# Attention and recurrent stage of a decoder layer: a scheduler's order, and one written out by hand

## The chip, the core and the metric

The kernel runs on one core of one Trainium2 chip. A core has a matrix engine (TensorE, PE in the profile; its weight loads are listed as PEld), VectorE (DVE), ScalarE (ACT), GpSimd (POOL) and SyncE (SP), which here only issues transfers (DMAs). Each engine works through its own list of instructions in order and waits on semaphores for the others. The metric is the device time of one execution in microseconds (us), the median of several runs.

## The reference, cut to what matters

One layer is computed for a prompt of 512 tokens and for 8 single decode tokens, so every activation has 520 columns here. Ahead of the second half of the layer (a mixer of experts, which the change does not touch) stand two branches that read the same normalized input `h`:

```
mods = jax.nn.silu(c) @ w_ada + b_ada
h = rms_norm(x, norm1_w) * (1 + sc1) + sh1
qa, ka, va, qh, fh, ih, gh, ga, gb = jnp.split(h @ w_in, IN_OFFSETS, axis=-1)
...
qa = rms_norm(qa.reshape(att_shape), q_norm_w) * (ATT_HEAD_DIM ** -0.5)
ka = rms_norm(ka.reshape(att_shape), k_norm_w)
att, kv_rows = attend(qa, ka, va)
f = lb + (1 - lb) * jax.nn.sigmoid(fh.astype(jnp.float32))
q_hg = jax.nn.silu(qh.astype(jnp.float32)).reshape(hg_k_shape)
k_hg = (1 - f).reshape(hg_k_shape)
logf = jnp.log(f).reshape(hg_k_shape)
o_hg, hg_state = recur(q_hg, k_hg, v_hg, logf)
o_hg = rms_norm(o_hg, hg_norm_w) * jax.nn.silu(gh.astype(jnp.float32).reshape(B, T, HG_HEADS, HG_DV))
y = jax.nn.sigmoid(ga) * (att @ w_br_a) + jax.nn.sigmoid(gb) * (hg @ w_br_b)
x = x + g1 * (y @ w_o)
```

`attend` is windowed attention in three groups of 8 heads of 64; `recur` is a gated linear recurrence with 8 heads of 128x128 state.

## The kernel before, in words

The product `h @ w_in` is done in column blocks of 128: 36 blocks for attention (four pairs of heads `hp`, three groups `g`, q, k and v), 32 for the recurrence (eight heads, each f, q, v and the output gate gg) and 16 for the two merge gates. One block, called a product here, is `proj`: a 512 KB weight tile `raw` is loaded, split into a rounded part `whi` (ACT, L129) and the rest `wlo` (DVE or POOL, L130), and 48 matmuls (8 chunks of the 1024 rows, three combinations, two halves of 260 columns) add up in a pair of PSUM banks (L177).

Stages, in order of time. First the modulation vectors and `h`. Then attention: for each head pair nine products, the norms of q and k (`norm_bc`: square on ACT, a rounded split, four matmuls, a square root on ACT, a reciprocal over 128x520 on DVE, L308, a multiplication), and eight slots (`r`, `hh`; L382 to L413). A slot computes scores with four matmuls S (L386 to L389), masks and takes their maximum on DVE (L392, L394), the exponential on ACT (L397), scales by the reciprocal sum (DVE, L400), transposes six pieces T (L404, L407) and multiplies with the values V (L411, L413). Sixteen blocks of the modulation weights (`mods`, "slabs", two half tiles each, L209 to L213) are given out beside the slots. Then the recurrence: each head's four products are followed by a chain: a logarithm, a running sum (`bb`), seven levels of decays (two subtractions L570, L571, an exponential L572, two multiplications L573, L574, matmuls L584, a masked copy L592), the state (L598 to L608), the decode states of 8 tokens on POOL (L617 to L619), the head's output `ob` and its norm. Decode attention (L417 to L475) stands once, before head 4. Last come the merge (`w_br_a`, `w_br_b`), `w_o` and the expert mixer.

Up to the mixer a scheduler sets each engine's order: it takes the program's order as priority and places instructions where it expects an engine to be free. From `order_.__enter__()` (L715) on, in the mixer, the engines' order is that of the program text (`manual_schedule`).

Of the kernel before, what the change touches and what calls it, by code (L numbers as in the profile page):

```python
# [36 lines left out]
MH = (0,) * 8  # L37
# [8 lines left out]
GT = ((0,),(1,),(2,),(3,),(),(4,),(5,),(6,))  # L46
GL = (7,)
# [3 lines left out]
NB_ = dict(sq=1, rs=2, shi=2, slo=2)  # L51
# [31 lines left out]
def layer(ctx, tc, A, O, K):  # L83
# [203 lines left out]
    def hblk(name):  # L287
        return hb.tile([P, N], F32, tag="hb", name=name, bufs=12)

    def wcol(c0):  # L290
        return A["w_in"][c0 // P]

    def norm_bc(x, lhsT, w, pl):

        sq, rs = pl("sq", F32), pl("rs", F32)
        act.activation(sq, x, AF.Square)
        parts = [sq]
        if lhsT.dtype == F32R:
            parts = pl("shi", F32R), pl("slo", F32R)
            split(*parts, sq, pool)  # L300

        def finish():
            for s in range(2):
                ps = bank("pn")
                for i, t in enumerate(parts):
                    pe.matmul(ps[:, :NH], lhsT, t[:, s * NH:(s + 1) * NH], start=i == 0, stop=i == len(parts) - 1)
                act.activation(rs[:, s * NH:(s + 1) * NH], ps[:, :NH], AF.Sqrt, bias=eps)
            dve.reciprocal(rs, rs)  # L308
            dve.scalar_tensor_tensor(out=x, in0=x, scalar=w, in1=rs, op0=ALU.mult, op1=ALU.mult)

        return finish
# [17 lines left out]

    with tc.tile_pool(name="at", bufs=2) as at:  # L330
# [9 lines left out]
        slabs = mods(range(8, 24))  # L340
        for hp in range(4):
            q, k, v, vtm = {}, {}, {}, {}
            for g in range(3):
                for t, dst, w in ((0, q, wq8), (1, k, col(C_K)), (2, v, None)):
                    ps = proj(wcol(t * 1536 + g * 512 + hp * P), KC, hT_hi, hT_lo)
                    x = at.tile([P, N], F32, tag="qkv", name="x", bufs=QKV)
                    act.activation(two(x), half(ps), AF.Copy)
                    if t:
                        finish()
                    if w is not None:  # L350
                        finish = norm_bc(x, bd, w, lambda n, dt: at.tile([P, N], dt, tag=n, name=n, bufs=NB_[n]))
                    dst[g] = x
# [27 lines left out]
            for r in range(4):  # L380
# [34 lines left out]
                for _ in range(MO[hp * 4 + r]):  # L415
                    next(slabs, None)
# [217 lines left out]
    for _ in slabs:  # L634
        pass
# [671 lines left out]
```

## Time and profile before

| | |
|---|---|
| median of 3 runs | 2489.33 us (2483.14 to 2490.37) |
| profiled execution, its own time | 2487.92 us |
| its span, first to last instruction | 2486.1 us |
| busy: PE, DVE, ACT, POOL | 94%, 71%, 46%, 30% of the span |
[...]
| first attention product leaves PSUM | 61.0 us after the span's start |
| first merge product with the recurrence's result | 989.0 us |

Busy PE is not the same as PE at its peak: matmuls overlap in the records, so a stretch can read as full while fewer matmuls go through it. The count of matmuls per stretch and the granted clock say more. [...]

### The profile page before, as it was taken

Reading aid. Unit: us, or ns where it says so; the run is one execution under the profiler, and the core shown is the slowest. Engines: PE = TensorE matmul, PEld = TensorE weight load, DVE = VectorE, ACT = ScalarE, POOL = GpSimd, SP = SyncE. Lnnn points to the kernel's source line nnn. Section 1 sums busy time; section 2 is a strip of 40 time slices with the busy share of each in tenths; the row PEclk is TensorE's granted clock in tenths of the full one; section 3 lists DMA queues with packets and bytes.
Section 4 is the critical chain, followed back from the end, with each engine's and each line's share of the span. In section 5 each row is a group of like instructions: output and inputs, shape, how many; then the busy total and the mean of one; then the engine's idle time right before and its main releaser. Section 6 shows DMA issues by size and latency. Waiting matters only on the chain.

```text
span 2486.1 us, 37938 instructions
## 1 busy us (share of the span) xinstructions
PE 2329.5 (94%) x14547; PEld 2133.4 (86%) x14547; DVE 1763.6 (71%) x3131; ACT 1155.2 (46%) x1801; POOL 738.1 (30%) x490
## 2 busy tenths in 40 slices
PE   8999999998897998999987989989999999999997
PEld 4869798888897998988987889978888888888886
DVE  4646573648786666536898897667888878788876
ACT  3545443555563555233336778733333333333332
POOL 1323120114227212002342000024454445454433
PEclk9989899999996998998998999989999999999999
DMA  7342421235443323432245456679999999999985
GB/s 243 110 141 92 132 89 44 71 96 166 150 126 103 115 91 100 154 105 95 78 129 186 180 187 225 227 272 349 335 349 336 356 329 342 341 348 331 345 298 208
DMA packets 197465, 495.49 MB, mean 199 GB/s; under 512 B 18122, under 2 KB 84650, under 8 KB 195748
## 3 DMA queue, kind: packets, MB, share of 16 engines
q1 hardware_dynamic: 147636, 313.02, 38.0%
q0 software_dynamic: 39456, 143.28, 16.1%
q10 hardware_dynamic: 10192, 36.77, 3.9%
q8 instruction: 114, 1.87, 0.3%
q14 instruction: 67, 0.55, 0.1%
HBM read 439.17 MB, written 54.49 MB: 199 GB/s over the span
## 4 chain that ended last, share of the span: by engine, by line
PE 36%; DVE 7%; issue 6%; ACT 3%; POOL 3%; DMA 1%; ACTq 0%; POOLq 0%; SPq 0%; DVEq 0%
PE acc L1186 16%; PE ph L809 14%; PE pp L177 3%; POOL gat L960 2%; PE pp L1071 2%; ACT oa L1063 1%; DVE wlo L130 1%; ACT whi L129 1%; DVE e L869 1%; ACT stage L1078 1%; DVE y L839 1%; DVE sel L871 0%; PE pt L895 0%; DVE oa L1057 0%; DVE e L866 0%
## 5 line engine op out<-in xcount | busy, mean ns | idle before, releaser
L130 DVE TENSOR_TENSOR wlo<-raw,whi 128x1024 fp32r<-128x1024 f32 (+1 forms) x238 | 293.9, 1236 | 198.5 <-ACT whi L129 196.9
L129 ACT ACTIVATE whi<-raw 128x1024 fp32r<-128x1024 f32 (+1 forms) x284 | 295.2, 1040 | 294.1 <-PE pp L177 168.3
L960 POOL DMA_INDIRECT gat<-in_peer_u,idx x128 | 212.6, 1661 | 627.1 <-DVE junk L987 442.0
L809 PE MATMUL ph<-h_hi,whi 128*128 128x384 f32 x1024 | 355.9, 348 | 15.1 <-ACT whi L129 15.1
L809 PE MATMUL ph<-h_hi,wlo 128*128 128x384 f32 x1024 | 351.6, 343 | 8.0 <-POOL wlo L130 7.3
L809 PE MATMUL ph<-h_lo,whi 128*128 128x384 f32 x1024 | 350.4, 342 | 0.0
L177 PE MATMUL pp<-hT_hi,whi 128*128 128x260 f32 x1344 | 292.5, 295 | 6.0 <-ACT hT_hi L129 4.8
L177 PE MATMUL pp<-hT_hi,wlo 128*128 128x260 f32 x1344 | 288.8, 294 | 1.9 <-DVE wlo L130 1.9
L177 PE MATMUL pp<-hT_lo,whi 128*128 128x260 f32 x1344 | 288.3, 294 | 0.5 <-DVE hT_lo L130 0.5
L177 PEld LDWEIGHTS pp<-hT_hi,whi 128*128 128x128 f32 x1344 | 218.5, 196 | 10.9 <-ACT hT_hi L129 4.9
L177 PEld LDWEIGHTS pp<-hT_hi,wlo 128*128 128x128 f32 x1344 | 218.2, 196 | 4.7 <-DVE wlo L130 2.1
L177 PEld LDWEIGHTS pp<-hT_lo,whi 128*128 128x128 f32 x1344 | 217.7, 197 | 3.5 <-issue 1.8
L809 PEld LDWEIGHTS ph<-h_hi,whi 128*128 128x128 f32 x1024 | 197.4, 193 | 19.5 <-ACT whi L129 16.7
L809 PEld LDWEIGHTS ph<-h_hi,wlo 128*128 128x128 f32 x1024 | 196.6, 192 | 10.2 <-POOL wlo L130 7.9
L809 PEld LDWEIGHTS ph<-h_lo,whi 128*128 128x128 f32 x1024 | 196.6, 192 | 2.8
L1186 PE MATMUL acc<-vhi,chi 128*128 128x512 f32 x768 | 195.8, 390 | 0.0
L1186 PE MATMUL acc<-vhi,clo 128*128 128x512 f32 x768 | 195.0, 389 | 0.0
L1186 PE MATMUL acc<-vlo,chi 128*128 128x512 f32 x768 | 194.9, 389 | 0.0
L130 DVE TENSOR_TENSOR vlo<-vr,vhi 128x1024 fp32r<-128x1024 f32 x128 | 156.2, 1220 | 52.9 <-ACT vhi L129 52.9
L129 ACT ACTIVATE vhi<-vr 128x1024 fp32r<-128x1024 f32 x128 | 135.3, 1057 | 114.7 <-PE acc L1186 114.7
L813 ACT ACTIVATE ge<-ph 128x384 f32<-128x384 f32 x128 | 62.6, 489 | 264.3 <-PE ph L809 263.9
L960 POOL DMA_INDIRECT gat<-in_peer_v,idx x128 | 162.7, 1271 | 70.9 <-issue 34.0
(375 smaller groups left out, 4688.9 us busy)
## 6 DMA issues: line engine op xcount, KB each, us to landing
raw<-in_uT SPq DMA_DIRECT2D x128, 512.0 KB
vr<-in_peer_v SPq DMA_DIRECT2D x128, 512.0 KB
raw<-in_w_in SPq DMA_DIRECT2D x84, 512.0 KB
raw<-in_w_ada SPq DMA_DIRECT2D x48, 512.0 KB
d_G<-stage ACTq DMA_DIRECT2D x12, 2048.0 KB
gt<-d_G SPq DMA_DIRECT2D x32, 768.0 KB
d_ge<-ge ACTq DMA_DIRECT2D x56, 192.0 KB
ge<-d_ge SPq DMA_DIRECT2D x56, 192.0 KB
```

The source lines that it names most:

```text
L129: act.activation(hi, src, AF.Copy)
L130: return (eng or dve).tensor_tensor(out=lo, in0=src, in1=hi.bitcast(F32), op=ALU.subtract)
L177: pe.matmul(ps[:, s, :NH], w[:, k, :], x[:, k, s * NH:(s + 1) * NH], start=first and n == 0, stop=last and n == 2)
L809: pe.matmul(ph[:, :NB], w[:, k], x[:, k, :NB], start=k == 0 and n == 0, stop=k == KC - 1 and n == 2)
L813: act.activation(ge, ph[:, :NB], AF.Gelu_apprx_tanh)
L839: dve.match_replace(out=y[:n], in_to_replace=vals[:, 0:8], in_values=x, imm_value=-3.0e38)
L869: dve.tensor_tensor(out=e3[:n], in0=e3[:n], in1=pb[:n, :, None, :].to_broadcast([n, H, 16, 16]), op=ALU.mult)
L960: pool.indirect_dma_start(out=t, out_offset=None, in_=A[tab][0], in_offset=bass.IndirectOffsetOnAxis(ap=idx, axis=0))
L1063: act.activation(oas[g][:, j], oas[g][:, j], AF.Copy, scale=sels[t][:, 0, n + j:n + j + 1])
L1071: pe.matmul(pgs[g // 2][:, g % 2, j * P:(j + 1) * P], oa[:, j], ob[:, j], start=True, stop=True)
L1078: act.activation(st[:, :, n0:n0 + 8], pgs.pop(b).rearrange("p s (n i) -> p i (s n)", i=P), AF.Copy)
L1186: pe.matmul(acc[2 * t + d], a[:, t * P:(t + 1) * P], b[:, d * 512:(d + 1) * 512], start=first and n == 0, stop=last and n == 2)
```

## The change

From the first attention product to the end of the recurrence the order is now the program's own (`flow = tc.manual_schedule`), and the program is written anew for it. A list `plan` names the weight tiles in the order of use; `weights_in` loads three tiles ahead and splits two ahead, always on ACT and DVE. Between any two products one step of other work is placed (`beside`): a slot of the previous head pair, divided into S in one step, T in the next and V after both heads; one norm's second part; or one of ten pieces of a recurrent head's chain, with the chains of two heads under way at once; beside them one or two steps of decode attention (`step_all`). Transfers of results are put off to the next step (`after`). The four first merge-gate blocks go between attention's last slots, the others into the heads, and none is left behind the recurrence.

Smaller edits go with it: sigmoid times x is computed as half of (tanh of half x plus 1) times x, where the halves go into later factors; `f` and `k` are made on ACT instead of DVE; the finest of the seven levels takes `f` itself (`neighbours`) and needs no decay; the decode states move from POOL (three operations of 128x1024 per head) to ACT and DVE (8 each of 128x128); the square root takes all 520 columns at once. Further on, where the mixer begins, the transposes that carry rows out are issued ahead of the matmuls that they used to interrupt, and their copies between ACT's other work.

```diff
-GT = ((0,),(1,),(2,),(3,),(),(4,),(5,),(6,))
-GL = (7,)
+
+
+G0 = 4
+GT = tuple((G0 + h,) for h in range(7)) + (tuple(range(G0 + 7, 16)),)
...
+    flow = tc.manual_schedule(engines={x.engine for x in (pe, dve, act, pool, dma)})
+    flow.__enter__()
...
+    for hp in range(4):
+        for n, (t, g) in enumerate(FIRST):
+            plan.append((acol(t, g, hp), KC))
+            if hp == 0 or hp == 1 and n < 7:
+                plan += slab_plan(8 + 9 * hp + n)
+    plan += [(hcol(i, 0), KC) for i in (1, 0, 2, 3)] + [(gcol(i), KC) for i in range(G0)]
+    for h in range(8):
+        plan += [(hcol(i, h + 1), KC) for i in (1, 0, 2, 3)] if h < 7 else []
+        plan += [(gcol(i), KC) for i in GT[h]]
...
+    def weights_in():
+
+        k = at_[2]
+        at_[2] += 1
+        while at_[0] < min(len(plan), k + 4):
+            src, kc = plan[at_[0]]
+            parts[at_[0]] = wtile("raw", F32, RAW)
+            dma.dma_start(parts[at_[0]].rearrange("p (k c) -> p k c", k=kc), src)
+            at_[0] += 1
+        while at_[1] < min(len(plan), k + 3):
+            hi, lo = wtile("whi", F32R, 3), wtile("wlo", F32R, 3)
+            split(hi, lo, parts[at_[1]])
+            parts[at_[1]] = [x.rearrange("p (k c) -> p k c", k=plan[at_[1]][1]) for x in (hi, lo)]
+            at_[1] += 1
+        return parts.pop(k)
+
+    def product():
+        return proj(None, KC, hT_hi, hT_lo, None, weights_in())
...
+    def beside():
+
+        begin()
+        for x in list(flows):
+            if next(x, 0) == 0:
+                flows.remove(x)
...
+            yield
+            for n in range(10):
+                if n >= 3 and n % 2:
+                    V((n - 3) // 2)
+                if 1 <= n < 9:
+                    T(n - 1)
+                if n < 8:
+                    S(n)
+                if n < 3:
+                    rows_of(hp, n)
+                yield
+
...
+        for hp in range(4):
+            flows.append(second_norms(hp))
+            for n in range(9):
+                beside()
+                if n == 8:
+                    next_ = slots(hp)
+                    next(next_)
+                qkv(hp, n)
+                if under:
+                    under()
+                    under = None
+                if hp == 0 or hp == 1 and n < 7:
+                    under = slab()
+            flows.append(next_)
...
+            def neighbours():
+
+                ws[6] = w = t2("w")
+                w4, q4, f4 = views(6, w, q, f)
+                dve.tensor_tensor(out=w4[:, :, 1], in0=f4[:, :, 1], in1=q4[:, :, 1], op=ALU.mult)
+
...
-            pool.tensor_tensor(out=ss, in0=ss, in1=f[:, NT:, None].to_broadcast([P, NS, P]), op=ALU.mult)
-            pool.tensor_tensor(out=vb, in0=vb, in1=k[:, NT:, None].to_broadcast([P, NS, P]), op=ALU.mult)
-            pool.tensor_tensor(out=ss, in0=ss, in1=vb, op=ALU.add)
...
+            for b in range(NS):
+                act.activation(ss[:, b], ss[:, b], AF.Copy, scale=f[:, NT + b:NT + b + 1])
...
+            for b in range(NS):
+                dve.scalar_tensor_tensor(out=ss[:, b], in0=vb[:, b], scalar=k[:, NT + b:NT + b + 1], in1=ss[:, b],
+                                         op0=ALU.mult, op1=ALU.add)
...
+        def step_all():
+            beside()
+            late_steps[0] += 1
+            for _ in range(2 if late_steps[0] % 4 == 0 else 1):
+                next(decode, None)
+
+
+        flows.append(chain(0))
+        beside()
+        beside()
+        for h in range(8):
+            for n, x in enumerate(([partial(part, h + 1, n) for n in ("f", "q", "v", "gg")] if h < 7 else []) + [partial(gate, i) for i in GT[h]]):
+                step_all()
+                x()
+                if h < 7 and n == 0:
+                    flows.append(chain(h + 1))
...
+    outs = [rows_out(d_g2, lambda c: modsT[:, 40 + c, :], 10), rows_out(d_xs, lambda c: xT[:, c, NT:], NS), x_tile(2), x_tile(3)]
...
-        if c in (1, 3):
-            rows_out(d_x[2 + c // 2], lambda c_: xT[:, c_, (2 + c // 2) * P:(3 + c // 2) * P], P)
-        elif c == 5:
-            rows_out(d_xs, lambda c_: xT[:, c_, NT:], NS)
-        elif c == 6:
-            rows_out(d_g2, lambda c_: modsT[:, 40 + c_, :], 10)
+        if c in (0, 2, 3, 4):
+            outs.pop({0: 2, 2: 2, 3: 0, 4: 0}[c])()
```

How the order changes, as the lists of the two programs print it (a row is an instruction, its result and operands, and how many stand in a run). First TensorE in the attention stage. In the kernel before, around a slot of the third head pair (`s_`: scores, `t_`: transposed pieces, `po`: the values' sum; `pp<-hT` is a product):

```order
926 L407 MATMUL t_2505<-ident,sm 128x64 x2
927 L386 MATMUL s_2592<-ks,qs 128x512
928 L387 MATMUL s_2592<-k_lo,qs 128x512
929 L177 MATMUL pp<-hT_hi,whi 128x260
930 L411 MATMUL po<-pt,vt 64x128 x2
931 L413 MATMUL po<-pt,vt 64x64 x3
932 L413 MATMUL po<-pt,vt 64x32
933 L389 MATMUL s_2593<-x 128x128 x2
934 L177 MATMUL pp<-hT_lo,whi 128x260 x2
```

In the change, one step of slots between two products (`pp<-shi`: the norm's matmuls):

```order
993 L180 MATMUL pp<-hT_hi,wlo 128x260 x2
994 L532 MATMUL t_2956<-ident,sm 128x128 x2
995 L535 MATMUL t_2956<-ident,sm 128x64
996 L535 MATMUL t_2956<-ident,sm 128x96
997 L535 MATMUL t_2957<-ident,sm 128x64 x2
998 L511 MATMUL s_2966<-ks,qs 128x512
999 L512 MATMUL s_2966<-k_lo,qs 128x512
1000 L514 MATMUL s_2967<-x 128x128 x2
1001 L383 MATMUL pp<-shi,bd 128x260
1002 L383 MATMUL pp<-slo,bd 128x260
```

What moved: before, a slot's matmuls are strewn between parts of a product; now a whole product (48) lies between a slot's scores and the transposes that need their result. Second, VectorE in one such step of the change (`ISA` is the masked maximum; `rs`, `x`: the norm of q; `wlo`: the weight split for two products on):

```order
325 L548 COPY att<-po 128x128
326 L537 COPY pt<-t_3792 128x128
327 L517 ISA sm,st_3808<-s_3801,m_378 128x512
328 L517 ISA st_3808 128x1
329 L519 ISA sm,st_3808<-s_3802,m_379 128x256
330 L519 ISA st_3808 128x1
331 L521 TENSOR_SCALAR st_3808<-st_3808 128x1
332 L524 RECIPROCAL rl<-st_3808 128x1
333 L525 TENSOR_SCALAR sm<-sm,rl 128x768
334 L385 RECIPROCAL rs<-rs 128x520
335 L386 SCALAR_TENSOR_TENSOR x<-x,cols,rs 128x520
336 L133 TENSOR_TENSOR wlo<-raw,whi 128x1024
```

Before, VectorE's list at a slot of the third head pair reads:

```order
241 L392 ISA sm,st_2599<-s_2592,m_376 128x512
242 L392 ISA st_2599 128x1
243 L414 COPY att<-po 128x128
244 L394 ISA sm,st_2599<-s_2593,m_377 128x256
245 L394 ISA st_2599 128x1
246 L396 TENSOR_SCALAR st_2599<-st_2599 128x1
247 L399 RECIPROCAL rl<-st_2599 128x1
248 L400 TENSOR_SCALAR sm<-sm,rl 128x768
249 L409 COPY pt<-t_2609 128x128
250 L130 TENSOR_TENSOR wlo<-raw,whi 128x1024
251 L392 ISA sm,st_2631<-s_2624,m_376 128x512
```

What moved: the reciprocal of a norm (128x520) now stands in the same step as a slot, behind the slot's scaling and ahead of the weight split. Third, TensorE in the recurrence. Before, beside head 1 (`pl<-w`: the levels):

```order
2010 L581 MATMUL pl<-w 64x64 x4
2011 L177 MATMUL pp<-hT_hi,wlo 128x260 x2
2012 L584 MATMUL pl<-w 128x64 x4
2013 L177 MATMUL pp<-hT_hi,whi 128x260 x2
2014 L177 MATMUL pp<-hT_lo,whi 128x260 x2
2015 L584 MATMUL pl<-w 128x64 x4
2016 L177 MATMUL pp<-hT_hi,wlo 128x260 x2
```

In the change, one step with the chains of two heads (levels and state of the one, transposes and diagonal of the next), between two products:

```order
2424 L180 MATMUL pp<-hT_hi,wlo 128x260 x2
2425 L761 MATMUL pl<-w,k 128x64 x4
2426 L846 MATMUL pkv<-vt,kt 128x128 x4
2427 L783 MATMUL pts<-ident,v 8x128
2428 L788 MATMUL ptm<-ident,v 128x128 x4
2429 L800 MATMUL pl<-q,k 128x128 x4
2430 L180 MATMUL pp<-hT_hi,whi 128x260 x2
```

What moved: before, one head's levels follow each other with two to four matmuls of a product between them; now one or two levels stand in a step, a whole product follows, and the next level comes after it.

## Rows read from the trace of the kernel before

**Rows 1.** Busy time by stretch: us, busy us (instructions) by engine, clock, DMA share.
```profile
61.00:182.00 121.00, 114.51 (x780) 96.09 (x779) 70.54 (x107) 61.19 (x97) 34.99 (x19) 0.90 0.41 128
296.00:460.00 164.00, 162.14 (x1177) 146.91 (x1175) 97.34 (x140) 77.66 (x131) 28.16 (x20) 0.99 0.20 61
545.00:982.90 437.90, 387.09 (x2950) 378.86 (x2948) 310.49 (x496) 240.32 (x293) 137.93 (x88) 0.91 0.39 124
61.00:989.00 928.00, 857.30 (x6227) 789.29 (x6227) 590.14 (x936) 482.62 (x675) 236.83 (x149) 0.93 0.35 109
```

**Rows 2.** The same view in three short stretches; engines PE, PEld, DVE, ACT, POOL.
```profile
260.00:280.00 20.00, 18.30 (x101) 12.64 (x101) 10.12 (x28) 9.75 (x15) 5.15 (x3) 0.74 0.40 133
400.00:420.00 20.00, 20.00 (x131) 16.63 (x130) 7.81 (x23) 5.69 (x10) 0.00 (x0) 1.00 0.08 27
840.00:860.00 20.00, 17.86 (x151) 17.08 (x150) 18.57 (x39) 10.82 (x14) 4.67 (x2) 1.00 0.25 91
```

**Rows 3.** Single lines: durations ns min/median/max, first and last start us.
```profile
L347 ACT ACTIVATE x<-pp x36: 581/586/605, 61.0 to 459.6; 128x520 f32<-128x520 f32 x36
...
L177 PEld LDWEIGHTS pp<-g_hi,whi x128: 187/188/193, 989.0 to 1054.5; 128*128 128x128 f32 x128
```

**Rows 4.** The chain that ended last: start us, us, what.
```profile
1126.44 8.55 PE pp L177 x48
...
1139.17 7.41 PE pp L177 x48
1147.47 5.74 PE pp L177 x48
```

**Rows 5.** TensorE's timeline around one slot: start us, us, line, count.
```profile
409.81 0.65 PE L411 MATMUL po<-pt,vt 128*64 128x128 f32 x4
...
410.83 0.62 PE L386 MATMUL s<-ks,qs 128*128 128x512 f32 x1
...
411.85 1.08 PE L389 MATMUL s<-x 64*128 64x128 f32 x4
...
415.85 0.38 PE L404 MATMUL t<-ident,sm 128*128 128x128 f32 x2
...
416.86 0.62 PE L386 MATMUL s<-ks,qs 128*128 128x512 f32 x1
```

**Rows 6.** Groups by line: count, busy us, mean ns, idle before and its releaser.
```profile
L129 ACT ACTIVATE whi<-raw 128x1024 fp32r<-128x1024 f32 (+1 forms) x284 | 295.2, 1040 | 294.1 <-PE pp L177 168.3
...
L308 DVE RECIPROCAL rs<-rs 128x520 f32<-128x520 f32 x32 | 108.3, 3393 | 16.2 <-ACT rs L307 16.1
...
L130 DVE TENSOR_TENSOR wlo<-raw,whi 128x1024 fp32r<-128x1024 f32 x99 | 127.4, 1289 | 81.8 <-ACT whi L129 80.3 <-PE pp L177 1.1
...
L392 DVE CUSTOM_DVE_ANT_0 sm<-s,m 128x512 f32<-128x512 f32 x32 | 21.9, 684 | 40.2 <-PE s L387 40.1
L400 DVE TENSOR_SCALAR sm<-sm,rl 128x768 f32<-128x768 f32 x32 | 19.9, 621 | 1.0
...
L397 ACT ACTIVATE sm<-sm,st 128x768 f32<-128x768 f32 x32 | 29.9, 934 | 75.5 <-DVE st L396 75.5
...
L397 ACT ACT_TABLE_LOAD x8 | 10.3, 1283 | 0.1
```

**Rows 7.** The recurrence's matmuls by line, and one row of TensorE's timeline.
```profile
L584 PE MATMUL pl<-w 128*128 128x64 f32 x384 | 63.3, 321 | 16.3 <-DVE w L574 15.1 <-ACT w L572 1.2
...
971.37 1.84 PE L623 MATMUL pos<-q,ss 128*128 128x1 f32 x16
```

**Rows 8.** VectorE's narrow operations: the group, and three rows of its timeline.
```profile
L571 DVE TENSOR_TENSOR w<-bb 128x256 f32<-128x256 f32 x56 | 38.5, 688 | 0.0
...
889.81 2.58 DVE L571 TENSOR_TENSOR w<-bb 128x256 f32<-128x256 f32 x1
...
892.99 0.41 DVE L570 TENSOR_TENSOR w<-bb 128x256 f32<-128x256 f32 x1
893.32 0.41 DVE L573 TENSOR_TENSOR w<-w,q 128x256 f32<-128x256 f32 x1
```

More of the change, by code (lines that the diff above doesn't have):

```diff
@@ new lines, in layer, with hblk, gate, part @@
+    at_.append(0)
+    heads = [{} for _ in range(8)]
+    hbs = [hb]
+    def hblk(h, name):
+        return hbs[h % 2].tile([P, N], F32, tag="hb", name=name, bufs=5)
+    def gate(i):
+        ps = product()
+        y = yblk("y")
+        act.activation(two(y), half(ps), AF.Tanh, scale=0.5)
+        after(lambda: dma2.dma_start(d_s[i // 2, i % 2], y))
+    def part(h, name):
+        x = heads[h][name] = hblk(h, name)
+        ps = product()
+        if name == "v":
+            act.activation(two(x), half(ps), AF.Copy)
+        elif name == "f":
+            act.activation(two(x), half(ps), AF.Sigmoid)
+            act.activation(x, x, AF.Identity, scale=oml[:, h:h + 1], bias=lb[:, h:h + 1])
+            k = heads[h]["k"] = hblk(h, "k")
+            act.activation(k, x, AF.Copy, scale=-1.0, bias=1.0)
+        else:
+            act.activation(two(x), half(ps), AF.Tanh, scale=0.5)
+            dve.scalar_tensor_tensor(out=two(x), in0=two(x), scalar=1.0, in1=half(ps), op0=ALU.add, op1=ALU.mult)
@@ new lines, in pairs, with rows @@
+                return placed
+            decays(0)
+            decays(1)
+            yield
+            v = d["v"]
+            pts = bank("pts")
+            pe.transpose(out=pts[:NS, :P], in_=v[:, NT:], identity=ident)
+            def rows(src, name):
+                pt = bank("ptm")
+                for i in range(4):
+                    pe.transpose(out=pt[:, i * P:(i + 1) * P], in_=src[:, i * P:(i + 1) * P], identity=ident)
+                dst = t2(name)
+                act.activation(dst, pt, AF.Copy)
+                return dst
@@ new lines, in chain @@
+            vs = hp_.tile([NS, P], F32, tag="vs", name="vs")
+            act.activation(vs, pts[:NS, :P], AF.Copy)
+            after(lambda: dma2.dma_start(d_hv[h], vs))
+            vt = rows(v, "vt")
+            pl = bank("pl")
+            for a in range(4):
+                c = slice(a * P, (a + 1) * P)
+                pe.matmul(pl[:, c], k[:, c], q[:, c], start=True, stop=True)
+            sides(0)
+            decays(2)
+            dve.tensor_mul(kd, kd, k[:, :NT])
+            am, qb = t2("am"), t2("qb")
@@ new lines, in chain @@
+            pk = bank("pkv")
+            for a in range(4):
+                c = slice(a * P, (a + 1) * P)
+                pe.matmul(pk[:, c], kt[:, c], vt[:, c], start=True, stop=True)
+            placed()
+            states = []
+            for a in range(4):
+                c = slice(a * P, (a + 1) * P)
+                new = hp_.tile([P, P], F32, tag="state", name="state", bufs=4)
+                if a:
+                    dve.scalar_tensor_tensor(out=new, in0=states[-1], scalar=eb[:, (a + 1) * P - 1:(a + 1) * P], in1=pk[:, c],
+                                             op0=ALU.mult, op1=ALU.add)
+                else:
+                    dve.tensor_copy(new, pk[:, c])
+                states.append(new)
```

534 lines of the change are left out of this document (312 added, 222 removed).

## The prediction

> **What bounds the kernel now.** I read the busy time by stretch first. From the first attention product that leaves PSUM (61.0) to the first merge product on the recurrence's result (989.0, [rows 3]) lie 928 us, over a third of the span, and all that is reordered. TensorE reads as busy for 857 us of them, but 6227 matmuls go through, one per 0.149 us, at a mean clock of 0.93 [rows 1]. Where nothing is in its way a product of 48 matmuls takes 5.74 us, 0.12 us each [rows 4], and the other matmuls here keep about that pace at their widths (sixteen one-column ones of the recurrence 1.84 us, [rows 7]; the 512-column scores are slower). So TensorE is the engine to fill, and it isn't filled. VectorE, 590 us busy of 928, and ScalarE, 483, are no bound over the whole stretch [rows 1]. Then single stretches: 61 to 182 us has 780 matmuls at clock 0.90 and ends with slots and slabs in the absence of products; 545 to 983 us, the recurrence, 2950 at 0.91 [rows 1]. In both the lists wait for one another: slot operations, levels and splits each follow a result of another engine. In 260 to 280 us, slots and slabs without products, the clock is 0.74, in 400 to 420 us, slots between parts of products, it is 1.00 [rows 2].
>
> **What TensorE has to do from there on.** 84 products at 5.74 us are 482 us. A slot is V, half of 410.83 - 409.81 = 1.02 us (the four and eight matmuls there serve two heads), S from 410.83 to about 412.8 (the last four start at 411.85 and take 1.08 us to their end), T from 415.85 to 416.86 [rows 5]: 0.5 + 2.0 + 1.0 = 3.5 us, 32 times 112 us. Each group of a head pair adds 0.65 us of transposes (seven at 0.09, estimated from the pace of the transposes in T), 12 times 8 us. A slab is 16 matmuls and two transposes, 2.2 us at the product's pace, 16 times 35 us; a norm of q or k four, 0.48 us, 24 times 11.5 us. A recurrent head: its levels are 384 / 8 = 48 matmuls in the trace [rows 7], the diagonal, state, state update, output and transposes about 54 more; 102 at 1.84 / 16 = 0.115 us [rows 7] are 11.7 us, the coarsest level, its norm and decode attention's share some 2.1: 13.8 us, eight times 110 us. Sum: 759 us. That is the floor; the order after can at best come near it.
>
> **The change, part by part.**
>
> Start. The first splits now stand behind the modulation in the lists; I allow 1 us: first product out at 62.
>
> First head pair (9 products, 9 slabs, no slots). By TensorE 5.74 + 2.2 + 0.48 = 8.4 us a step. But ScalarE's list after a product is: evacuate, square, round, then the split of the next product's weights (1.04 us), then VectorE's rest (1.29, [rows 6]). Three passes over 520 columns at 0.6 us (estimated from 0.93 for 768, [rows 6]) make 1.8 + 1.04 + 1.29 = 4.1 us behind the product, of which 0.3 is saved because four matmuls need only the rounded weights: 5.74 + 3.9 = 9.6 us. 9 x 9.6 = 86, at 148 us.
>
> Second head pair (slots of the first, seven slabs). In a step with slot, norm and slab VectorE goes, from the scores on: maxima 0.68 and about 0.4 for half the width, 0.93 for the exponential on ScalarE, scaling 0.62, then the wait for the square root (table load 1.28 + 0.6, less the 0.62), reciprocal 3.39, norm and small ones about 1, split 1.29 [rows 6]: 9.5 us until the second half slab's weights are there. TensorE has norm, product and first half slab, 7.2 us, in that time; then half a slab and V, T, S: 9.5 + 0.95 + 3.5 = 13.9 us. Five such steps; two without a norm 12.0 each (TensorE's sum), one without a slab 9.9, one with only T 6.8: 70 + 41 = 111, at 259.
>
> Third and fourth. A step with slot and norm is 5.74 + 3.5 + 0.48 = 9.7 on TensorE and, by the list above with copies of 0.5, about 10 on VectorE; I take 9.9. Per pair 6 x 9.9 + 9.9 + 8.9 + 6.8 = 85; both 170, at 429. Then 8 products (head 0's four, four gates) beside the last slots at 9.2: 74, at 503.
>
> Change-over. Buffers of attention are given back, and head 0 must run Ln, sum, decays and two levels' factors before any product may follow in TensorE's list: last T and V, table load and Ln 2, some 8 us of VectorE: 12 us idle, and 5 for a clock that has fallen. At 520.
>
> Recurrence, 40 products. TensorE needs 28.7 + 13.8 = 42.5 us per head with five products. VectorE per head: 25 narrow operations (12 subtractions left of 14, 12 multiplications of 14, one new). They take 0.41 us undisturbed and start 0.33 apart, but 0.69 in the mean, with single ones of 2.58 [rows 8]. Five splits 6.5, reciprocal 3.4, eight state updates at about 0.33 (like the narrow ones), the rest (sum, products over 512 columns, masked copies, decode sums; some twenty operations, estimated at 0.65 between narrow and 768 wide) about 13: 26 + 25 x 0.33 = 34 us at best, 26 + 17 = 43 at the present mean. ScalarE, busy for about half of the stretch [rows 1], lies beside. So TensorE bounds, with VectorE close. In the step order each level's factors are made a step ahead of its matmuls; by those sums VectorE stays ahead, except at a norm (its reciprocal comes after square root and table load), where it has 5 us of slack per head. 40 x 5.74 + 8 x 13.8 = 340, and 3% for steps that don't fit: 350, at 870.
>
> [...]
>
> End. After the last product head 7's norm stands alone: 7 us (square root, reciprocal, two multiplications), then 6 us of splits as before: at 883. Clock: 0.93 over 928 us [rows 1] is 130 us at half rate; with products in every step, as in 400 to 420 us [rows 2], I expect some 12 us, costing 6. The first merge product on the recurrence comes at 889 instead of 989: 100 us gained.
>
> Mixer's beginning. The first product there takes 8.55 us at a reduced clock, and the second starts 12.7 us after it [rows 4], behind transposes that wait for copies. With those ahead, and the extra column add moved to ScalarE, I take 6 us; bounds 0 and 10. Everything behind it is the same program.
>
> Weight loads: each tile is asked for three tiles ahead, over 17 us; the queue that issues them now also holds last step's results, which are then there. I price it at nothing; its cover is TensorE's two or three products.
>
> **Sum.** 2487.9 (the profiled execution) - 106 = 2382 us. The median is 1.4 us above the profiled time, so the same figure stands for it within its error.
>
> **The rivals.**
>
> A. TensorE's floor is reached: 62 + 759 + 12 + 5 + 13 = 851 and 6 at the mixer: 2344 us; a few us lower if the change-over hides. For it: VectorE has room by its undisturbed times. Against: the 9.6 and 13.9 us loops, which follow from ScalarE's and VectorE's lists.
>
> B. The lists hold each other up. If VectorE's present mean (43 us a head) and its waits add up without overlap, a step of the recurrence takes 9.5 us instead of 8.7, one of attention 11 instead of 9.9, with slab 15.5 and 10.6: 62 + 95 + 124 + 198 + 84 + 17 + 380 + 13 + 6 = 979, and 2472 us. For it: VectorE reads 18.6 of 20 us busy where two levels and splits meet (840 to 860, [rows 2]). Against: TensorE still passes 151 matmuls there at full clock.
>
> C. The clock falls through all steps (slower). Place: the pauses of 1 to 3 us before products in every step. [...] For it: 0.74 in 260 to 280 us though TensorE reads 18.3 of 20 busy. [...] Against: 840 to 860 us has gaps of over 2 us and clock 1.00 [rows 2].
>
> D. Nothing changes, because the scheduler's order was already as dense as the waits allow: 296 to 460 us reads 162 of 164 [rows 1]. But that is one stretch of three; within 0.3% of before has little room.
>
> **Chances.** My forecast (2350 to 2420) 0.60; A 0.13; B, 2420 to 2480, 0.16; C 0.08; D 0.03. The range 2340 to 2450 takes in the forecast, most of A and half of B, about 0.8. A change of 0.3% (7 us) is about what can be told from none here. Faster 0.88, same 0.03, slower 0.09.
>
> **What would show it.** The first merge product on the recurrence at about 889 us; steps of 9.6, 13.9 and 9.9 us in attention, from product to product; heads 43 to 45 us apart in the recurrence with TensorE at over 160 matmuls per 20 us; mean clock over the stretch 0.97 or more; VectorE's narrow operations nearer 0.45 than 0.69 us; an idle stretch of about 12 us where the recurrence begins. It would be wrong if a transfer or a PSUM bank's reader, neither of which I price, holds a step, or if the clock of [rows 2]'s first stretch comes back between products.

## The result, and the profile after

The changed kernel takes 2455.61 us (median of four, 2451.89 to 2459.33) against 2486.23 for the kernel before beside it: a ratio of 0.9866, 95% interval 0.984 to 0.9893. It is faster, by 31 us (1.3%) and not by the forecast's 106, and lies above the forecast's range of 2340 to 2450. The profiled execution has a span of 2451.9 us against 2486.1.

Where the 34 us of the two spans lie: the first merge product with the recurrence's result (`g_hi`) starts at 964.5 and not at 989.0 ([rows 3]), 24.5 us; a single matmul of it stands ahead, beside the first merge product on attention's result (`a_hi`), which starts at 959.3. TensorE's rows (start us, us, line, count):

```profile
959.28 0.80 PE L180 MATMUL pp<-a_hi,whi 128*128 128x260 f32 x2 [7.68 <-ACT a_hi L132]
959.88 0.42 PE L180 MATMUL pp<-g_hi,whi 128*128 128x260 f32 x1
...
964.55 0.28 PE L180 MATMUL pp<-g_hi,whi 128*128 128x260 f32 x1
```

The mixer's second product starts at 1107.9, against 1139.17 ([rows 4]): from the merge to there 143.4 us for 150.2, another 6.8. Behind it 2.9 us. So the mixer's edits gave about the 6 us that were forecast, and the shortfall of 75.5 us (100 forecast, 24.5 measured) stands ahead of 964.5. By TensorE's timeline (starts of the next stage's first product; the fifth row is the end of the product itself):

| stage ends at | forecast | measured |
|---|---|---|
| first head pair | 148 | 149.3 |
| second head pair | 259 | 265.8 |
| fourth head pair | 429 | 449.9 |
| eight products beside the last slots | 503 | 531.0 |
| last product of the recurrence | 870 | 949.9 |
| first merge product on the recurrence | 889 | 964.5 |

28 us are lost in attention and 52 from the change-over to the last product; behind it 4.4 are won. The view of busy time by stretch, as in [rows 1] (us, then busy us and instructions of PE, PEld, DVE, ACT and POOL, granted clock, DMA share, GB/s); the fourth row ends 2.8 us into that merge product, the last is the new recurrence:

```profile
61.00:182.00 121.00, 112.67 (x858) 100.70 (x856) 84.67 (x97) 69.09 (x100) 16.93 (x12) 0.99 0.50 163
296.00:460.00 164.00, 164.00 (x1194) 149.76 (x1193) 109.30 (x171) 105.44 (x144) 28.22 (x18) 0.98 0.19 60
545.00:982.90 437.90, 388.27 (x3009) 380.62 (x3010) 293.33 (x515) 212.54 (x335) 100.01 (x68) 0.92 0.39 128
61.00:967.30 906.30, 839.55 (x6303) 786.62 (x6302) 594.37 (x975) 483.08 (x715) 162.50 (x111) 0.94 0.35 113
...
531.00:951.40 420.40, 373.35 (x2900) 365.46 (x2898) 281.74 (x509) 207.69 (x327) 92.93 (x64) 0.92 0.40 130
```

The profiler's records of the granted clock, as shares of full speed, take only two values in both kernels, 1.00 and 0.50 (half clock, below): 29 records of each before, 32 of each after. A 128x260 matmul of a product started 0.120 us after the one before it at 1.00, and 0.217 at 0.50 (medians, 0.218 before), so that some 0.45 of a time at half clock is lost. The mean over the execution is 0.962, and 0.955 before.

From 61 us to the merge the clock has barely changed (0.94 for 0.93), and the recurrence still passes only 2900 matmuls in 420 us, 138 per 20 us, where more than 160 were expected. VectorE is busy for 67% of it and ScalarE for 49%: no engine is full. What TensorE waits for there (the view of waits from 531 to 967, which takes in the 7.7 us ahead of the merge: us in total, times, longest):

```profile
PE pts L783 <- ACT v L434: 26.4, 7, 5.4
PE pp L180 <- ACT a_hi L132: 7.7, 1, 7.7
PE pl L761 <- DVE w L740: 7.4, 8, 1.9
PE ptm L788 <- issue: 5.6, 1, 5.6
PE pl L761 <- DVE w L746: 3.6, 3, 2.7
PE pc L654 <- DVE pr L650: 2.0, 1, 2.0
PE pc L641 <- DVE sc L635: 1.3, 2, 1.0
PE pkv L846 <- DVE am L773: 0.5, 1, 0.5
```

Half of it is one wait: in each of seven heads the transposes of v stand for ScalarE to take v out of PSUM. Why v is late is read from the timelines of one head, ScalarE's list first (start us, us, line; in brackets the idle time before and its releaser), then rows of VectorE's and TensorE's:

```profile
799.37 0.69 ACT L384 ACTIVATE rs<-pp,eps 128x520 f32<-128x520 f32 x1
...
810.01 0.63 ACT L735 ACTIVATE w<-w 128x512 f32<-128x512 f32 x1 [1.98 <-DVE w L734]
810.55 1.04 ACT L132 ACTIVATE whi<-raw 128x1024 fp32r<-128x1024 f32 x1
811.61 1.28 ACT L436 ACT_TABLE_LOAD   x1
812.90 0.60 ACT L436 ACTIVATE f<-pp 128x520 f32<-128x520 f32 x1
...
814.94 2.43 ACT L828 ACTIVATE ss<-ss,f 128x128 f32<-128x128 f32 x8
817.37 1.28 ACT L713 ACT_TABLE_LOAD   x1
818.67 0.63 ACT L713 ACTIVATE lf<-f 128x512 f32<-128x512 f32 x1
...
820.26 1.28 ACT L441 ACT_TABLE_LOAD   x1
821.56 0.60 ACT L441 ACTIVATE q<-pp 128x520 f32<-128x520 f32 x1
827.05 0.63 ACT L721 ACTIVATE kd<-kd 128x512 f32<-128x512 f32 x1 [4.88 <-DVE kd L720]
...
830.09 0.58 ACT L434 ACTIVATE v<-pp 128x520 f32<-128x520 f32 x1
```

```profile
800.10 3.40 DVE L385 RECIPROCAL rs<-rs 128x520 f32<-128x520 f32 x1 [8.07 <-ACT rs L384]
803.54 0.91 DVE L386 SCALAR_TENSOR_TENSOR ob<-ob,half_w,rs 128x520 f32<-128x520 f32 x1
...
806.96 0.41 DVE L734 TENSOR_TENSOR w<-bb 128x256 f32<-128x256 f32 x1
...
808.48 1.50 DVE L734 TENSOR_TENSOR w<-bb 128x256 f32<-128x256 f32 x1
...
822.20 0.69 DVE L442 SCALAR_TENSOR_TENSOR q<-q,pp 128x520 f32<-128x520 f32 x1 [0.52 <-ACT q L441]
...
823.15 2.18 DVE L836 SCALAR_TENSOR_TENSOR ss<-vb,k,ss 128x128 f32<-128x128 f32 x8
825.25 1.25 DVE L773 COPY_PREDICATED am<-lv,pl 128x256 f32<-128x256 uint8 x2
826.30 0.71 DVE L720 TENSOR_TENSOR kd<-bb 128x512 f32<-128x512 f32 x1
```

```profile
825.72 1.16 PE L846 MATMUL pkv<-vt,kt 128*128 128x128 f32 x8 [0.53 <-DVE am L773]
830.72 0.33 PE L783 MATMUL pts<-ident,v 128*8 128x128 f32 x1 [3.84 <-ACT v L434]
```

The product of v is done by 824.4, but its copy stands in ScalarE's list behind exponentials that wait for VectorE's `kd`, which stands behind the decode states, behind q's gate, which waits for ScalarE's tanh, behind the states' scaling and a logarithm, behind f. From f's copy to v's, 812.90 to 830.09, it is one chain of 17.2 us back and forth between two engines that are both far from full; in the seven heads that wait it is 17 to 25 us. From the end of f's product (805.9) to the end of v's copy (830.7) are 24.8 us, and TensorE runs out of work after 21.0 (826.9). And f itself was late: its product ended at 805.9, but the copy stood behind exponentials that waited for decays behind the norm's reciprocal.

### The profile page after: what moved, and what is told of

The parts are those of the page before. It is cut to its first block, busy times and chain, and to the rows that moved or that the text cites. A ratio compares the mean times of both kernels' runs of the same rounds, so it can differ in the third digit from the quotient of the medians.

```text
span 2451.9 us, 37852 instructions
## 1 busy us (share of the span) xinstructions
PE 2297.9 (94%) x14547; PEld 2118.4 (86%) x14547; DVE 1760.3 (72%) x3156; ACT 1155.0 (47%) x1850; POOL 660.6 (27%) x450
## 4 chain that ended last, share of the span: by engine, by line
PE 43%; DVE 7%; ACT 3%; DMA 1%; issue 1%; ACTq 0%; POOL 0%; POOLq 0%; DVEq 0%; SPq 0%
PE acc L1471 21%; PE ph L1091 16%; PE pp L180 3%; PE pp L1356 2%; ACT oa L1348 1%; DVE wlo L133 1%; ACT whi L132 1%; DVE e L1151 1%; ACT stage L1363 1%; DVE y L1121 1%; DVE sel L1153 0%; PE pt L1177 0%; DMA vr<-in_peer_v 0%; DVE oa L1342 0%; DVE e L1148 0%
## 5 line engine op out<-in xcount | busy, mean ns | idle before, releaser
L133 DVE TENSOR_TENSOR wlo<-raw,whi 128x1024 fp32r<-128x1024 f32 (+1 forms) x254 | 320.0, 1265 | 176.4 <-ACT whi L132 175.2
L180 PE MATMUL pp<-hT_hi,whi 128*128 128x260 f32 x1344 | 287.9, 297 | 17.2 <-ACT whi L132 17.1
L180 PE MATMUL pp<-hT_hi,wlo 128*128 128x260 f32 x1344 | 280.0, 291 | 5.1 <-DVE wlo L133 5.1
L180 PE MATMUL pp<-hT_lo,whi 128*128 128x260 f32 x1344 | 279.7, 291 | 0.0
```

The lines of the kernel that those rows point to most:

```text
L133: return (eng or dve).tensor_tensor(out=lo, in0=src, in1=hi.bitcast(F32), op=ALU.subtract)
L180: pe.matmul(ps[:, s, :NH], w[:, k, :], x[:, k, s * NH:(s + 1) * NH], start=first and n == 0, stop=last and n == 2)
```

## The experiments

Ratios are to the kernel before, run beside each; its median was 2486.7 to 2493.3 us from one group of runs to another, so differences of a few us between kernels of different groups are read from the ratios too. Without other words an edit is made on the changed kernel. A run's clock and waits are those of its one profiled execution.

**v first.**
```
-                step_all()
-                x()
+                young = flows.pop() if h < 7 and n == 2 else None
+                step_all()
+                x()
+                if young:
+                    next(young)
+                    flows.append(young)
```


> One step of the recurrence is reordered: in the step of v the young head's second piece (its decay to the end of the chunk, the first two levels' decays) is written behind the product of v and not ahead of it, so that ScalarE takes v out of PSUM ahead of that piece's exponentials, which wait for VectorE. Nothing else changes. Theory 1: the recurrence falls short of the forecast because TensorE waits for v at its transposes (26.4 us in seven waits in the changed kernel), and each such wait is followed by half clock. Then the waits for v fall below 1 us each, the stretch from 531 to 952 us gets 25 to 45 us shorter, and the time is 2410 to 2430 us. Rival: VectorE's list is what is late; the same time is then waited for by the next levels' products: 2450 to 2460 us.


Measured 2450.32 us, 0.9839 (0.9813 to 0.9865): in the rival's range and not to be told from the changed kernel; theory 1 in this form fell. TensorE no longer waits for v; it waits a little later in the same step, for the PSUM bank of the next matmuls, which VectorE's masked copy gives back:
```profile
PE pl L800 <- DVE am L773: 17.3, 6, 4.1
```
So v's place in one list was not the cause. VectorE is late at the same place.

**States on GpSimd.**
```
-                act.activation(ss[:, b], ss[:, b], AF.Copy, scale=f[:, NT + b:NT + b + 1])
+            pool.tensor_tensor(out=ss, in0=ss, in1=f[:, NT:, None].to_broadcast([P, NS, P]), op=ALU.mult)
```
(and `vb` times k and the sum as two more on `pool`.)


> One part of the change undone: the decode tokens' states are updated again by three 1024-wide operations on GpSimd (1.9, 2.8 and 2.4 us in the kernel before) and not by eight short ones on ScalarE (2.43 us per head) and eight on VectorE (2.18). They stand in the same steps as now. Theory 1: both lie on the chain that ends with v's evacuation, so each wait for v shortens by up to 4.6 us: 20 to 30 us gained, 2425 to 2440 us. Rival: the changed kernel gains by having them off GpSimd, since VectorE's operations beside GpSimd's take longer: 2455 to 2475 us.


Measured 2460.94 us, 0.9888 (0.9867 to 0.9908): in the rival's range, though theory 1's wait does shrink. The waits for v fall from 26.4 to 10.9 us, and those for the levels rise from 7.4 to 23.3, because VectorE's operations get longer. TensorE's two waits, and three of VectorE's groups in the recurrence (count, busy us, mean ns):
```profile
PE pl L761 <- DVE w L740: 23.3, 9, 6.7
PE pts L783 <- ACT v L434: 10.9, 5, 3.3
```
```profile
L740 DVE TENSOR_TENSOR w<-w,k 128x256 f32<-128x256 f32 x48 | 34.2, 712 | 0.0
L739 DVE TENSOR_TENSOR w<-w,q 128x256 f32<-128x256 f32 x48 | 33.8, 704 | 0.0
...
L385 DVE RECIPROCAL rs<-rs 128x520 f32<-128x520 f32 x7 | 23.8, 3403 | 39.5 <-ACT rs L384 39.5
```
In the changed kernel L740 takes 433 ns and L739 495 in the mean; the reciprocal takes 3403 in both. The records of this run can be parted by whether a GpSimd operation ran at the same time: L740 then takes 1.98 us in the mean (9 cases) and 0.42 without (39), the reciprocal 3.40 either way (3 and 4). What sets the one apart from the other was not tried. Some of it is left in the changed kernel, where decode attention's products run on GpSimd beside the heads: from 520 to 990 us the two subtractions (L733, L734) take 1.27 us in the mean where a GpSimd row overlaps theirs (8 cases) and 0.42 where none does (88). In the head shown above one takes 0.41 us at 806.96 and 1.50 at 808.48, beside the row below. How much of TensorE's waits comes from that was not tried.
```profile
808.35 1.34 POOL L674 TENSOR_TENSOR tap<-tap 128x512 f32<-128x512 f32 x1
```

**No reciprocal.**
```
-            dve.reciprocal(rs, rs)
+            if lhsT.dtype == F32R:
+                dve.reciprocal(rs, rs)
```


> Leaves out the reciprocal of the recurrent heads' norms (3.40 us on VectorE, eight times), so the heads are scaled by the root instead. It tests the step of the forecast that gave VectorE 5 us of slack per head there. Theory 1: the norm starts the chain that ends with the late v, so 3.4 us off it take about 3 us off each wait: 20 to 35 us gained with the clock, 2420 to 2437 us. If the forecast's step held, it is hidden: 2450 to 2458 us but for 3.4 us at the last head.


(The heads' results are then scaled by the root itself; only the time is read.) Measured 2426.45 us, 0.9751 (0.9732 to 0.977): 29 us, so the reciprocal is not hidden, and the slack of 5 us that the forecast gave it did not exist. But not as theory 1 had it: the waits for v stay at 24.6 us, and it is those behind the norm that vanish (L761, in the changed kernel two rows with 11.0 us; here, one line further down, 1.4):
```profile
PE pts L784 <- ACT v L435: 24.6, 7, 5.5
...
PE pl L762 <- DVE w L747: 0.9, 2, 0.6
PE pl L762 <- DVE w L741: 0.5, 1, 0.5
```
So there are two chains per head: one behind the norm, one from f to v. A wait that is as long when everything ahead of it comes earlier is set by the chain inside its own steps.

**f by tanh.**
```
-            act.activation(two(x), half(ps), AF.Sigmoid)
+            act.activation(two(x), half(ps), AF.Tanh, scale=0.5)
```
(with `oml` halved and added to `lb`.)


> The forget gate by a tanh with the scale and bias halved, as the other gates are, and not by a sigmoid: one of ScalarE's table loads (1.28 us) less in each of seven heads. Theory 1: the load lies on the chain to v's evacuation: 7 x 1.28 = 9 us, with the clock up to 12: 2443 to 2448 us. Rival: ScalarE waits for VectorE ahead of it and behind it, and the load is hidden: 2453 to 2458 us.


Measured 2446.49 us, 0.9833 (0.9816 to 0.9849): 9 us, in theory 1's range, so the loads are not hidden though ScalarE is idle half of the time. That it is just 7 x 1.28 is partly chance: in the profiled executions the recurrence is 10.1 us shorter, of which TensorE's waits make 4.5 (42.3 for 46.8); where the rest comes from was not shown.

**States later.**
```
-            for b in range(NS):
-                act.activation(ss[:, b], ss[:, b], AF.Copy, scale=f[:, NT + b:NT + b + 1])
             sides(4)
...
             for x in placed:
                 x()
+            for b in range(NS):
+                act.activation(ss[:, b], ss[:, b], AF.Copy, scale=f[:, NT + b:NT + b + 1])
             yield
```
(and VectorE's eight from that step to the end of the next.)


> The decode states' eight operations on ScalarE are written one step later, those on VectorE too; the operations and engines are those of the changed kernel. Theory 1 now reads: from the end of f's product to v in SBUF runs one chain through ScalarE's and VectorE's lists (f, its two maps, the states' scaling 2.43, Ln, split, q, q's product with its gate, the states' 2.18, masked copies, decay, exponentials, split, v), about 20 us with its table loads, and TensorE has about 16 us of work in that time. Then 4.6 us off the chain end the waits for v (26.4 us): 20 to 35 us gained with the clock, 2420 to 2435 us. Rival: as with v written first, another wait takes most of it, for a PSUM bank behind VectorE's masked copies or for the levels: 2445 to 2455 us.


Measured 2432.38 us, 0.9774 (0.9748 to 0.98): 23 us by moving the same instructions one step on. From f's copy to v's it is now 13.0 us (799.46 to 812.42 in that head), 4.2 less, and
```profile
PE pts L783 <- ACT v L434: 9.4, 5, 3.3
PE pl L761 <- DVE w L740: 7.8, 8, 1.6
```
This bears out theory 1 in its second form: the chain from f to v, over both lists, is what makes the waits for v, the longest of TensorE's.

**Norms by Ln and Exp.**
```
-            act.activation(two(rs), half(ps), AF.Sqrt, bias=eps)
-            dve.reciprocal(rs, rs)
+            act.activation(two(rs), half(ps), AF.Ln, bias=eps)
+            act.activation(rs, rs, AF.Exp, scale=-0.5)
```


> All norms of q, k and the heads by Ln and Exp on ScalarE in place of its square root and VectorE's reciprocal (3.40 us). For the heads alone leaving the reciprocal out gave 29 us; 0.65 us more on ScalarE each takes 5 of it: 24 gained there. Theory 1: in attention TensorE waits little for VectorE (4.5 us for the slabs' second halves): 2 to 6 us more, 2422 to 2432 us. Rival: the attention steps that came out longer than forecast (hp 2 and 3: 10.2 us and not 9.9) are also set by VectorE's list: 10 us more, 2412 to 2420 us.


Measured 2443.75 us, 0.9817 (0.9783 to 0.9851). It is a miss of both. Attention ended 6 us earlier (the recurrence's first product at 524.8 for 531.0), as theory 1 said: in the profiles with the norms as they were it starts at 528.5 to 536.9, with Ln and Exp, and attention otherwise as it was, at 524.6 to 527.9. But the recurrence itself took 425.5 us for 428.3 (to the first merge product): of the 24 us next to nothing. The second table load, which used to lie beside the reciprocal, now stands ahead of the result (ScalarE's timeline, then VectorE's first row behind it), so that the head is scaled 2.67 us after the first map starts, for 4.17 in the changed kernel (799.37 to 803.54): 1.5 us less per head, where 2.75 were expected. TensorE's waits fell by 2.5 us only (44.3 for 46.8), and the recurrence had more half clock (92 us for 78.5):
```profile
789.72 0.69 ACT L384 ACTIVATE rs<-pp,eps 128x520 f32<-128x520 f32 x1
790.43 1.28 ACT L385 ACT_TABLE_LOAD   x1
791.72 0.64 ACT L385 ACTIVATE rs<-rs 128x520 f32<-128x520 f32 x1
792.39 0.96 DVE L386 SCALAR_TENSOR_TENSOR ob<-ob,half_w,rs 128x520 f32<-128x520 f32 x1 [8.48 <-ACT rs L385]
```

**A filler ahead of v's transposes.**
```
+            for _ in range(14 if h else 0):
+                pe.matmul(pts, hT_hi[:, 0, :P], hT_hi[:, 0, :512], start=True, stop=True)
```


> Adds 14 matmuls of 128 x 512 on data that is long there ahead of v's transposes in seven heads (some 3.3 us at full clock each, into a bank that the transposes then overwrite); nothing is taken away. If the half clock behind the waits comes from TensorE standing still in them, the half-clock stretches behind v's waits (some 37 us) go and their cost of some 12 us is gained: 2440 to 2448 us. If it comes from something else: 2453 to 2462 us.


Measured 2452.52 us, 0.9854 (0.9826 to 0.9882): not to be told from the changed kernel, 0.5 us under the range of "something else". By the trace's records of the granted clock, half clock from the recurrence's first product to the first merge product on its result fell from 78.5 to 51.2 us, and the recurrence from 428.3 to 421.4. So half clock fell by 27.3 us, most of the 37 that the first theory named (in the changed kernel six of the seven waits for v have half clock in them or right behind them, 37.5 us; the first, 0.56 us long, has none), without the theory's gain in time: the profiled execution's attention, the same program, ended 5.6 us later, and the filler is work too (128x512 matmuls at full clock started 0.227 us apart in the kernel before, L1186; at that pace fourteen are 3.2 us, an estimate). The mean clock of all four executions rose, 0.965 to 0.969 for 0.960 to 0.963.

**Three together** (states later, Ln and Exp, tanh).


> Three edits together: states later, norms by Ln and Exp, f by tanh. Theory 1, with waits that add up: 29 + 28 + 9 less what they share; TensorE's work of 337 us in the recurrence and 5 us per wait that stays set the bound: 2385 to 2405 us. Rival: another wait takes their place after the first: 2415 to 2425 us.


Measured 2403.59 us, 0.9664 (0.9639 to 0.969): theory 1. The recurrence takes 381.4 us, and its heads come 47 us apart for 54; the clock (third number from the end) is 0.96 for 0.91 in the changed kernel, first row:
```profile
531.00:959.30 428.30, 373.57 (x2901) 365.60 (x2899) 287.24 (x514) 210.38 (x331) 92.93 (x64) 0.91 0.40 132
```
```profile
524.60:906.00 381.40, 354.44 (x2900) 347.66 (x2899) 262.98 (x506) 206.04 (x332) 92.60 (x64) 0.96 0.46 149
```

**Two of the three** (without Ln and Exp).


> The states later and f by tanh, with the norms as in the changed kernel (square root on ScalarE, reciprocal on VectorE). It shows what the norms' edit is worth behind the other two, after it gave 3 us in the recurrence alone. If the waits behind the norms count again once the chain from f to v is short: 2415 to 2424 us, 12 to 20 us above the three together (2403.6). If the norms' edit gives only what it gave in attention: 2407 to 2412 us.


Measured 2421.95 us, 0.9723 (0.9683 to 0.9762): 18 us more than with three, 14 if each is set against the kernel before beside it. The norm's edit, worth 3 us in the recurrence alone, is worth 15 there behind the other two (396.4 us for 381.4). TensorE's waits ahead of the merge are 25.9 us for 20.8, so 5 of the 15 are waits; the clock is 0.94 for 0.96, some 17 us more at half clock, which at the 0.45 above are 8 of the rest, an estimate.

**A later start, and v first with it.** `beside()` once and not twice behind `flows.append(chain(0))`, on the three; then v first as well.


> The three edits, and one more: head 0's chain begins one step later against the products, so that head 1's first product stands between its sum and its first decays. The wait of 6.4 us for the decayed keys behind head 1's first product, and the 10 us of half clock there, come from the chain's start (two constants' transfers, the sum, the decays) with only one product beside it. If so, 5 to 10 us less than with three edits: 2394 to 2399 us. Rival: the wait moves to the next step: 2401 to 2406 us.

> As the run before it, and the young head's second piece behind v's product too. Of the waits for v 6.6 us are left in the kernel with three edits. If VectorE no longer stands ahead of the PSUM bank that took the wait's place when this was tried alone: 4 to 8 us less than without it. Rival: the bank's wait comes back: no change or up to 5 us more.


Measured 2416.1 us (0.9699, 0.9659 to 0.9738) and 2411.43 (0.9681, 0.9636 to 0.9725): 12 and 8 us more than the three, 8 and 3 against the kernel before beside each. The first miss is outside both theories: the wait got 2.3 us shorter, a new one of 2.9 us stands a step on, and half clock rose from 30.7 to 54.6 us. The second is 4.7 us below the first, as its first theory says, but its four runs (2405 to 2417) take in the first's; the wait a step on is 8.1 us there.

**The end.** `G0 = 3` for 4, on the later start.


> As the second run of this group, with three gate products beside the last attention slots and not four, and so six behind head 6. Head 7's norm then has a product beside it. At the end of the recurrence TensorE stood 6.2 us before the merge: if the norm and what is behind it made that wait, 3 to 6 us less than without it. Rival: the wait is for the last sum of the decode attention, and the slots at the other end lose a product beside them: no change to 5 us more.


Measured 2416.66 us, 0.9706 (0.9666 to 0.9747): no change, as the rival says. The wait ahead of the merge fell from 6.2 to 1.1 us, as the first theory says, but the last slots, without a product beside them, wait 2.8 us for VectorE, and the 45th product starts 4 us later (530.3 for 526.2).

**The clock again**: v first on the three; the filler (8 matmuls) on the later start; the filler on the three.


> The three edits (states later, norms by Ln and Exp, f by tanh) and the young head's second piece behind v's product. If the later start was what cost the two runs with it 8 to 12 us, and v first gives what it gave beside it (5 us): 2396 to 2401 us. If the bank behind VectorE takes the wait over and the half clock comes with it: 2404 to 2415 us.

> The kernel with three edits and the later start (2416.1), with 8 matmuls of 128 x 512 on data long there ahead of v's transposes in seven heads, 1.9 us at full clock each, 13 us in all; the waits for v there were 7.8 us in five. If the 54.6 us at half clock in its recurrence come behind these waits: half clock falls to about 30, and the time by 3 to 8 us in spite of the added work, 2408 to 2413 us. If not: the added work shows, 2418 to 2428 us.

> The three edits (2403.6) with the same filler. There half clock is 30.7 us, and none of it stands behind waits for v: the filler's 13 us less the 6.6 us of waits that it fills are added, 2407 to 2413 us. If the clock gains here too: 2398 to 2404 us.


Measured 2406.84 us (0.9673, 0.9652 to 0.9693), 2418.0 (0.9712, 0.9693 to 0.9732) and 2416.18 (0.9697, 0.9672 to 0.9722). Half clock: 30.7, 44.4 (from 54.6) and 54.6 us (from 30.7). The first lies in the second theory's range, but half clock did not come with it: the bank's wait (5.1 us) took the place of v's (6.6). The second is at the lower edge of "the added work shows", with some of the half clock gone. The third is above both ranges: the filler takes the waits for v away (0.3 us are left), and in these two profiles half clock grows all the same. That the filler makes it grow is not shown: the profiles are the fastest execution of the three edits and the slowest of this run, and over four executions each the mean clock is 0.968 to 0.973 and 0.966 to 0.972. So a filler lowered half clock in two kernels, and in the third only its added work shows; how far these waits set the clock, and what else does, stays open.

## Why the prediction missed

**The step that failed** is the recurrence's: "TensorE bounds, with VectorE close", "ScalarE ... lies beside", "5 us of slack per head", and so 3% for what doesn't fit. The sums were right: TensorE's work (420.4 us less 46.8 of waits and half of the 68 at half clock leave about 340, the forecast's 340), VectorE busy for 281.74 / 8 = 35 us per head (forecast 34 to 43), narrow operations of 0.43 to 0.50 us for 0.69 in [rows 8]. But a sum per engine says nothing about a result that passes through two in-order lists several times. Seven heads had a chain of 17 to 25 us from f's copy to v's, and the heads a second one behind the norm; TensorE's list had too little between their ends. The forecast allowed 27 us for idle time, its clock and misfits from the change-over on; measured are 46.8 us of waits up to 951 (the rows above without `a_hi`) and 68 us at half clock up to there (0.92 over 420.4), of which at most half, 34, is lost. How much of the half clock comes from the waits stays open. Experiments bear it out: 23 us back from moving the states, 9 from a table load, 29 from leaving out the reciprocal, 52 from the three edits that keep the result.

**The clock.** Forecast: 12 us at half rate in all. Measured: 0.94 over 906.3 us, by the records 107.6 us at 0.50, which cost up to 54 against the 6 in the sum. The 12 us were an estimate from one good stretch of [rows 2], taken for all of them. As in rival C the clock fell, but in part of the steps only, and a gain of 31 us was left.

**Attention**, 28 us late, is TensorE-bound as forecast, without waits in the third and fourth pair. A term was mis-sized: V. A step in the changed kernel:
```profile
384.44 0.65 PE L545 MATMUL po<-pt,vt 128*64 128x128 f32 x4
...
386.18 0.44 PE L532 MATMUL t<-ident,sm 128*128 128x128 f32 x2
...
387.25 0.63 PE L511 MATMUL s<-ks,qs 128*128 128x512 f32 x1
...
389.28 0.39 PE L383 MATMUL pp<-shi,bd 128*128 128x260 f32 x1
```
V takes 1.74 us here for two slots (384.44 to 386.18; 24 records, two for each of a slot's six matmuls), 0.87 each. The forecast halved the 1.02 us of [rows 5] because it took the twelve records there for two heads; they are one's. 32 x 0.37 = 12 us. A norm takes 0.59 us (389.28 to the next product at 389.87) and not 0.48, 24 x 0.11 = 3; the clock, 0.97 from 61 to 530, up to 14. The three make about the 28.

**What held.** The first pair (90 us for 86); the change-over cost 4 us of matmuls, without idle time, ahead of its first product (526.9 to 531.0, in the fourth row of the table) and a wait of 5.6 behind it, for 17 (its 5 us for a fallen clock were an estimate that no row showed; measured are 10.2 us at half clock, from 540.7); the end 14.6 us for 19; the mixer 6.8 for 6, by the mechanism that was named, since TensorE's waits for copies of transposed rows fell from 8.7 to 2.9 us, but ahead of the first product and not between the first two, which are 12.3 us apart for 12.7; weights and transfers for next to nothing: ScalarE's splits wait 5.2 us for raw tiles in attention and 1.8 in the recurrence. The start did not hold: the first attention product leaves PSUM at 67.1 and not at 62 (61.0 before), because it starts only at 59.2, behind a wait of 14.5 us for its split weights; the table's starts don't show it. A PSUM bank's reader, which was named as a way to be wrong, takes over only once v is moved.

**The rivals.** B, the lists hold each other up, is what happened, at 0.16; its price for the recurrence, 380 us, was still 40 too low, because it stretched VectorE's durations and not the waiting between the lists. That the measured time falls into B's 2420 to 2480 is partly luck: in attention its price is 30 us too high (501 us for the 472 measured from the first product to 531), because the later pairs do not wait for the lists at all.

## What to carry to other kernels

In an order written by hand, follow each value from the product that makes it to the matmul that needs it through every list it passes, table loads and what stands ahead of it included, and set that latency against TensorE's work in between: low busy shares are no slack. Work that nobody waits for (here the decode states) belongs behind what somebody does, and one step's move can be worth more than a faster operation. Count what a row serves before a duration is divided by it.

## What the runs showed of the hardware

Edits that leave TensorE's work alone moved the time at half clock in the recurrence between 30.7 and 92 us (the largest with the norms by Ln and Exp alone). At the 0.45 of such a time that is lost by the pace of a product's matmuls (0.217 us for 0.120), the 24 us between the later start (54.6) and the three edits (30.7) are 11 us, an estimate, of the 8 to 12 by which the two differ. One program's clock differs from run to run as well: with the three edits its mean was 0.968 to 0.973 in four executions, and where attention is the same program it ended between 528.5 and 536.9 us, with 19 to 39 us of it at half clock.

With the decode states on GpSimd the VectorE multiplication of 128x256 (L740) took 0.42 us, and 1.98 in the mean beside a GpSimd operation; the reciprocal of 128x520 took 3.40 us in either case. A table load took ScalarE 1.28 us.
